# adaLN row sums by a reduction that turns 32 x 32 blocks on VectorE, and a group norm sum in single-pass products

## The chip, the cores and the metric

One core of one Trainium2 chip runs the whole program. The metric is device time in microseconds, lower is better. The kernel before took 1380.81 us, the median of 3 runs (1379.1 to 1381.97).

## What is computed

A trunk of two layers on x (512 tokens x 1024). Layer 0 mixes tokens with a gated short convolution, layer 1 with a Mamba-2 SSD mixer in 8 groups; a SwiGLU feed-forward layer (FFN) follows each. So there are four sub-layers, s = 0 to 3, and each is wrapped like this:

```
mod = (silu(c) @ ada_w + ada_b).reshape(bsz, DEPTH, 2, 3, D_MODEL)
shift, scale, gate = ...                            # of sub-layer s
h = rmsnorm(x, g_pre) * (1 + scale) + shift
x = x + gate * rmsnorm(mixer_or_ffn(h), g_post)
```

`ada_w` is 1024 x 12288 and c is one vector: a product of one row, whose 12288 results the kernel wants as columns (feature on partitions), 96 columns of 128 in `mods`. Inside the SSD mixer, y is normalised by groups of 256 features: `rms_normalize(y.reshape(bsz, s, g, 256))`. Everything is fp32.

## The kernel before

**Products.** All large products run as three single-pass products of 512 tokens each, on operands that are split in a high part (rounded to the reduced type fp32r) and the rest: lines 262, 263 and 264 of the input products, for example. ScalarE makes the high part of a weight and VectorE the rest (`split_w`, L202 and the line after it; L221 where the split is put later). A product of plain fp32 operands, as in the transposes of small things, the C-B products of the SSD and the sum of the group norm, is made of several passes by the compiler.

**Weights.** SP issues the loads of weights into a staging tile (`wst`, two buffers; L211 and L229), from which the two engines split them into `whl` (four buffers). At the end of each sub-layer, `load_lead` (L245) brings the first weights of the next one ("lead weights"), so that TensorE can start behind the boundary. The same SP queue issues the loads of `ada_w`.

**adaLN.** The first 16 columns of `mods` (shift and scale of sub-layer 0) come from products at the start (`ada_pe`, L184). The other 80 come from VectorE, in 20 sets of 512 columns of `ada_w` (`ada_set`). For a set, SP loads four tiles of 128 x 2 x 512 (`ada_st`, L134, three buffers); VectorE multiplies each 128 x 512 half by the value of silu(c) of its partition and adds it to an accumulator `ada_acc` (L124 the first, L126 the seven behind it; two buffers). What is left is a sum over the 128 partitions. `ada_finish` makes it: four transposes of 128 x 128 on TensorE (L119) put the accumulator into PSUM with features on partitions, and VectorE reduces over the free dimension (L120) and adds `ada_b`. `ada_fin` then makes the columns that are used: (1 + scale) times the pre-norm's weight (`acol`) and gate times the post-norm's (`gcol`). `ada_next(n)` finishes the set begun at the call before and begins n new ones. It is called with 2 in three of the four steps of the convolution layer, and 14 sets in all from nine steps of the first FFN; none is left behind that.

**Small vectors.** `other_vectors` loads four small vectors by rows with DMAs issued by ScalarE, and turns each into columns with a transpose (`ptr`, L91) and a copy. It is called in the third step of the convolution layer. `put_gates` (`ggp`) turns the gates of a sub-layer into rows; for sub-layers 1 to 3 that happens in the FFN's step f = 18.

**Group norm of the SSD.** For each of 8 groups, `step_c` makes two tiles `y0` of 128 features x 512 tokens. ScalarE squares each; VectorE adds the second square to the first (`accg`, L1133). `sums` lets TensorE sum `accg` over the partitions with a matrix of ones in plain fp32 (`ssg`, L1144), ScalarE takes the root (L1148), VectorE the reciprocal (L1152) and scales. `sums` stands about seven input products behind `step_c`.

**Order.** The instructions of each engine run in order. Mostly a scheduler places them, by the times at which it thinks buffers come free; so a buffer that is freed by another engine moves the loads behind it on SP, and the work on them.

**The boundary** at the end of a sub-layer: the last output products end, ScalarE squares (`xn<-y`, L411) the last rows, the norm follows, and TensorE turns the normalised rows (`xtr`, L478) into the next sub-layer's input. The lead weights' splits stand ahead of those squares on ScalarE.

Of the kernel before, what the change touches and what calls it, by code (L numbers as in the profile page):

```python
# [8 lines left out]
F32 = mybir.dt.float32  # L9
# [7 lines left out]
P = 128  # L17
T = 512
# [17 lines left out]
def trunk_kernel(  # L36
# [57 lines left out]
    def other_vectors(stage):  # L94
        d_rows = stage[:16, 3, :].rearrange("p (a b) -> p a b", b=HD)
        d16 = stage[:16, 4, 0:2]
        dma_s(stage[0:16, 0, :], m_norm_g.rearrange("i (r p) -> (i r) p", p=P))
        dma_s(stage[:32, 1, :], m_conv_b.rearrange("i (r p) -> (i r) p", p=P))
        dma_s(stage[:, 2, :], m_conv_w.rearrange("i k (r p) -> (i k r) p", p=P))
        dma_s(d16, m_d.rearrange("i (r p) -> (i r) p", p=2))  # L100
        turned(stage[:, 0, :], mng, 16)
# [3 lines left out]
        turned(d_rows.rearrange("p a b -> p (a b)"), dcol, 16)  # L105

    mods = consts.tile([P, 96], F32, name="mods")
    acol = consts.tile([P, 32], F32, name="acol")
# [2 lines left out]

    xt = [hp.tile([P, D], F32, name=f"x{t}", tag=f"x{t}") for t in range(4)]


    def ada_finish(acc, ncol, dst):
        n = ncol // P
        pt = aux_ps("ada_ps")
        for b in range(n):
            pe.transpose(pt[:, b * P:(b + 1) * P], acc[:, b * P:(b + 1) * P], ident)  # L119
        dve.tensor_reduce(dst, pt[:, :ncol].rearrange("p (a b) -> p a b", b=P), axis=AX.X, op=ADD)  # L120

    def ada_madd(acc, w, k):
        if k == 0:
# [12 lines left out]
                ada_madd(acc, st[:, k, :], kh * 2 + k)  # L136
        return acc

    def ada_fin(col0, acc):
# [4 lines left out]
        kind, j = divmod(r, 8)  # L144
        if kind == 1:
            dve.scalar_tensor_tensor(acol[:, s * 8 + j:s * 8 + j + 4], mods[:, q:q + 4], 1.0,
                                     ncol(s, 0, j, 4), ADD, MUL)
        elif kind == 2:
            dve.tensor_mul(gcol[:, s * 8 + j:s * 8 + j + 4], mods[:, q:q + 4], ncol(s, 1, j, 4))

    def ncol(s, post, j, n=1):
        i, sub = divmod(s, 2)
# [398 lines left out]
    ada_open = []  # L551
# [12 lines left out]
    with ExitStack() as ph:  # L564
        ada_p.append(ph.enter_context(tc.tile_pool(name="adap", bufs=3, reuse_waits="tile")))
        actp = ph.enter_context(tc.tile_pool(name="actp", bufs=22, reuse_waits="tile"))
        gx = ph.enter_context(tc.tile_pool(name="gx", bufs=1, reuse_waits="tile"))

        def act_tile(name):
            return actp.tile([P, 2, T], F32R, tag="a", name=name)  # L570
# [268 lines left out]
        def ffn(s, i, begun, act_tile, gg_tile, xn_tile, ada, gates, lead, after):  # L839
# [13 lines left out]
            for f in range(0, NF, 2):  # L853
# [9 lines left out]
                for b in range(2):  # L863
                    ff_act(pss[b], pss[2 + b], f + b)
                ada(f)
                if f == 18:
                    for q in gates:
                        put_gates(q)
                    gg = make_gg(s, gg_tile)
# [9 lines left out]
                    ssd_lead, lambda: load_w([(wm_in, P, P)]))  # L879
        h, lead_ps, rest, wz1 = begun  # L880

        assert not ada_sets and not ada_open


    with ExitStack() as ph:
# [99 lines left out]
        class Group:  # L985
# [120 lines left out]
            def step_c(self, q):  # L1106
# [23 lines left out]
                else:  # L1130
                    sqg = t2("sqg")
                    act.activation(sqg, y0, AF.Square)
                    dve.tensor_add(self.accg, self.accg, sqg)  # L1133
                ygs.append(y0)

            def step_d(self):
                self.sums()
                self.root()
                self.norm()

            def sums(self):

                self.ssg = aux_ps("ssg")
                pe.matmul(self.ssg, ones, self.accg, start=True, stop=True)  # L1144

            def root(self):
                self.rg = t2("rg")
# [34 lines left out]
        with tc.manual_schedule(engines={PE_ENGINE, mybir.EngineType.Activation, mybir.EngineType.DVE}):  # L1182
# [67 lines left out]
            next(conv2[3])  # L1250
            next(conv2[3])
            next(conv2[2])
            next(conv2[3])
            nn.split(1)
            nxt.project_z(0)
# [5 lines left out]
            for g in range(1, NG - 1):  # L1261
# [38 lines left out]
                if nn:  # L1300
                    nn.later[0][1]()
                    nn.split(1)
                next(conv2[3])
                nxt.project_z(0)
                if nn:
                    nn.weights(1)
# [81 lines left out]
```

## Time and profile before

| | |
|---|---|
| median of 3 runs | 1380.81 us |
| the profiled execution's own time | 1383.75 us |
| span of its profile | 1382.0 us |
| granted TensorE clock | 0.998 |
| opening, to the first product of the adaLN | 11.5 us |
| transposes of the first boundary (convolution layer to FFN) | from 206.3 us |
| first FFN | about 206 to 578 us |
| SSD layer's groups | 40.8 us from one group norm sum to the next |

The profile is of one execution, which had a time of its own; its span is what the trace covers, 1.75 us less. Times in the rows are in us from the span's start. PE is TensorE, PEld its weight loads, DVE VectorE, ACT ScalarE, POOL GpSimd, SP the engine that issues the loads. In a row of a group, `out<-in` names tiles (buffer numbers left out), `xN` is the number of instructions, and behind the bar stand busy time, mean ns of one, and the idle time ahead of them with what ended it. In a row of the timeline stand start, duration, engine, line, the operation and, in brackets, the idle time ahead of it and what ended it. Matmuls are pipelined, so their durations overlap; what one costs is read from the starts of its neighbours.

### The profile page before, as it was taken

To read this page: it belongs to the slowest core of one execution; us is meant where nothing else is said; L and a number is where in the kernel's file an instruction comes from. 1 tells how busy PE (TensorE), PEld (TensorE's weight loads), DVE (VectorE), ACT (ScalarE), POOL (GpSimd) and SP (SyncE) were. 2 spreads that over 40 slices of the span, in tenths; PEclk is the share of its full clock that TensorE was granted. 3 is DMA by queue.
4 is the path that set the end of the run, shared out by engine and by line. 5 is a ranking of instruction groups with operands and counts; after the bars stand their busy time and mean duration, and the time that the engine had idled before them with its cause. 6 is when DMAs were issued, how large, how long until landed. Compare 5 with 4: busy or idle time off the path is not lost.

```text
span 1382.0 us, 17400 instructions
## 1 busy us (share of the span) xinstructions
PE 1366.8 (99%) x7035; PEld 1147.2 (83%) x7035; DVE 841.6 (61%) x1331; ACT 535.4 (39%) x817; POOL 1.5 (0%) x11
## 2 busy tenths in 40 slices
PE   8999999999999999999999999999999999999998
PEld 7788879888888888898888888888888888888886
DVE  5887756487775222759988898897573333332224
ACT  5432256222222211745555445564472322222112
POOL 0000000000000000000000000000000000000000
PEclk9999999999999999999999999999999999999999
DMA  9966661368773223415343423313403223322221
GB/s 313 328 205 230 211 211 62 122 213 268 237 257 122 92 92 102 116 47 172 107 138 109 136 84 115 128 57 121 154 30 107 92 93 113 99 92 92 92 92 62
DMA packets 154181, 190.36 MB, mean 138 GB/s; under 512 B 5860, under 2 KB 111220, under 8 KB 153076
## 3 DMA queue, kind: packets, MB, share of 16 engines
q1 hardware_dynamic: 149952, 176.34, 39.8%
q10 hardware_dynamic: 4148, 12.90, 2.9%
q8 instruction: 55, 0.90, 0.3%
q14 instruction: 26, 0.21, 0.1%
HBM read 186.98 MB, written 2.24 MB: 137 GB/s over the span
## 4 chain that ended last, share of the span: by engine, by line
PE 65%; DMA 1%; DVE 1%; ACT 1%; issue 0%; DVEq 0%; ACTq 0%
PE ip L262 11%; PE ip L264 11%; PE ip L263 11%; PE y L362 7%; PE y L364 7%; PE y L363 7%; PE li L262 2%; PE li L264 2%; PE li L263 2%; PE yd L1118 1%; DMA wst<-in_f_w_in_dram 1%; PE yo L1112 1%; PE xtr L478 1%; PE cb L1057 1%; PE xtok L1040 1%; PE st L1073 0%
## 5 line engine op out<-in xcount | busy, mean ns | idle before, releaser
L262 PE MATMUL ip<-h,whl 128*128 128x512 f32 x1096 | 433.2, 395 | 0.0
L264 PE MATMUL ip<-h,whl 128*128 128x512 f32 x1096 | 427.2, 390 | 0.0
L263 PE MATMUL ip<-h,whl 128*128 128x512 f32 x1096 | 426.8, 389 | 0.0
L262 PEld LDWEIGHTS ip<-h,whl 128*128 128x128 f32 x1096 | 205.8, 188 | 44.1 <-issue 2.6
L263 PEld LDWEIGHTS ip<-h,whl 128*128 128x128 f32 x1096 | 205.9, 188 | 43.2 <-issue 1.4
L264 PEld LDWEIGHTS ip<-h,whl 128*128 128x128 f32 x1096 | 205.7, 188 | 43.3
L203 DVE TENSOR_TENSOR whl<-wst,whl 128x1024 fp32r<-128x1024 f32 (+1 forms) x127 | 133.5, 1070 | 105.9 <-ACT whl L202 105.7
L202 ACT CAST whl<-wst 128x1024 fp32r<-128x1024 f32 (+1 forms) x127 | 114.8, 926 | 202.6 <-PE ip L264 117.1
L203 DVE TENSOR_TENSOR whlo<-wsto,whlo 128x1024 fp32r<-128x1024 f32 x68 | 83.0, 1224 | 176.4 <-ACT whlo L202 176.2
L202 ACT CAST whlo<-wsto 128x1024 fp32r<-128x1024 f32 x68 | 71.2, 1051 | 197.5 <-PE y L364 158.8
L362 PE MATMUL y<-whlo,ff 128*128 128x512 f32 x352 | 137.0, 389 | 0.0
L364 PE MATMUL y<-whlo,ff 128*128 128x512 f32 x352 | 136.9, 389 | 0.0
L363 PE MATMUL y<-whlo,ff 128*128 128x512 f32 x352 | 136.9, 389 | 0.0
L126 DVE SCALAR_TENSOR_TENSOR ada_acc<-ada_st,csil,ada_acc 128x512 f32<-128x512 f32 x140 | 104.9, 749 | 20.0 <-DMA ada_st<-in_ada_w_dram 17.1
L262 PE MATMUL li<-h,whl 128*128 128x256 f32 x288 | 83.4, 290 | 0.0
L847 DVE TENSOR_TENSOR g<-ip,g 128x512 f32<-128x512 f32 x40 | 27.6, 690 | 90.2 <-PE ip L264 90.2
L264 PE MATMUL li<-h,whl 128*128 128x256 f32 x288 | 81.5, 283 | 0.0
L263 PE MATMUL li<-h,whl 128*128 128x256 f32 x288 | 81.5, 283 | 0.0
L846 ACT ACTIVATE g<-ip 128x512 f32<-128x512 f32 x36 | 21.5, 598 | 144.7 <-PE ip L264 144.7
L363 PEld LDWEIGHTS y<-whlo,ff 128*128 128x128 f32 x352 | 66.1, 188 | 13.8
L362 PEld LDWEIGHTS y<-whlo,ff 128*128 128x128 f32 x352 | 66.1, 188 | 13.7
L364 PEld LDWEIGHTS y<-whlo,ff 128*128 128x128 f32 x352 | 66.1, 188 | 13.6
(215 smaller groups left out, 1688.9 us busy)
## 6 DMA issues: line engine op xcount, KB each, us to landing
ada_st<-in_ada_w_dram SPq DMA_DIRECT2D x96, 512.0 KB, 5.7
wst<-in_f_w_in_dram SPq DMA_DIRECT2D x44, 1024.0 KB, 5.2
wsto<-in_f_w_out_dram SPq DMA_DIRECT2D x20, 1024.0 KB, 5.1
wst<-in_m_w_in_dram SPq DMA_DIRECT2D x14, 1024.0 KB, 5.3
wst<-in_m_w_in_dram SPq DMA_DIRECT2D x20, 512.0 KB, 4.2
wst<-in_a_w_in_dram SPq DMA_DIRECT2D x9, 1024.0 KB, 7.1
csb<-cs_d ACTq DMA_DIRECT2D x8, 1024.0 KB, 7.2
wsto<-in_m_w_out_dram SPq DMA_DIRECT2D x7, 1024.0 KB, 5.0
```

The costliest lines, as they stand in the source:

```text
L126: dve.scalar_tensor_tensor(acc, w, csil[:, k:k + 1], acc, MUL, ADD)
L202: act.copy(dst[:, 0, :nk, :], src)
L203: dve.tensor_tensor(dst[:, 1, :nk, :], src, dst[:, 0, :nk, :].bitcast(F32), SUB)
L262: pe.matmul(dst, w_at(w, 0, kk), a[:, 0, sl], start=start, stop=False)
L263: pe.matmul(dst, w_at(w, 0, kk), a[:, 1, sl], start=False, stop=False)
L264: pe.matmul(dst, w_at(w, 1, kk), a[:, 0, sl], start=False, stop=stop)
L362: pe.matmul(pst, a[:, 0, tk], wt[:, 0, kk, :], start=k == 0, stop=False)
L363: pe.matmul(pst, a[:, 0, tk], wt[:, 1, kk, :], start=False, stop=False)
L364: pe.matmul(pst, a[:, 1, tk], wt[:, 0, kk, :], start=False, stop=k == K - 1)
L478: pe.transpose(pt[:, j * 256 + t * P:j * 256 + (t + 1) * P], self.xn[2 * hi + t][p // 2][:, c:c + P], ident)
L846: act.activation(g, psg, AF.Silu)
L847: dve.tensor_mul(g, psu, g)
```

## The change

Three things are changed. Lines are those of the new kernel where the rows below are of it.

**adaLN.** `ada_finish` with its four transposes is gone. `ada_fold` reduces the accumulator on VectorE with `apply_transpose`: it views the 512 columns as 16 blocks of 32, turns each 32 x 32 block and sums it, so that row 32g + i, column b of the result holds the sum over the 32 partitions of quarter g, of accumulator column 32b + i. Two sets (1024 columns, one kind of one sub-layer) fill a tile `fold` of 128 x 32. What is left is the sum of four quarters: one plain fp32 product of `fold`, 32 columns, with `four`, a matrix that is 1 where row and column agree modulo 32 (four unit matrices added by GpSimd). Four additions of 32 partitions each put the result with `ada_b` into `mods`. `acol` and `gcol` are made for 8 columns at once instead of 4. `ada_next` finishes a pair of sets at the call behind the one that completed it.

**Small vectors.** `other_vectors` becomes a generator: its DMAs are issued in the convolution layer as before, its transposes stand in the first FFN at step f = 4. The gates of sub-layers 1 to 3 are put at f = 20 instead of 18.

**Group norm.** For groups 0 to 6 the second square is added by GpSimd instead of VectorE. `split_sq` splits `accg` as other operands are: ScalarE rounds it (`sqs`), VectorE takes the rest; and `sums` makes two single-pass products with `ones_r`, a rounded copy of the ones that ScalarE makes at the program's start. Group 7 stays as it was.

```diff
+    ones_r = consts.tile([P, P], F32R, name="ones_r")
+    act.copy(ones_r, ones)
...
-    def ada_finish(acc, ncol, dst):
-        n = ncol // P
-        pt = aux_ps("ada_ps")
-        for b in range(n):
-            pe.transpose(pt[:, b * P:(b + 1) * P], acc[:, b * P:(b + 1) * P], ident)
-        dve.tensor_reduce(dst, pt[:, :ncol].rearrange("p (a b) -> p a b", b=P), axis=AX.X, op=ADD)
...
+    def ada_fold(acc, dst):
+        dve.tensor_reduce(dst, acc.rearrange("p (b r) -> p b r", r=32), axis=AX.X, op=ADD, apply_transpose=True)
...
-        ada_finish(acc, 512, mods[:, q:q + 4])
-        dve.tensor_add(mods[:, q:q + 4], mods[:, q:q + 4], adab[:, q:q + 4])
+        pt = aux_ps("ada_ps")
+        pe.matmul(pt[:, :32], four, part, start=True, stop=True)
+        for b in range(4):
+            r = slice(b * 32, (b + 1) * 32)
+            dve.tensor_tensor(mods[r, q:q + KD], pt[r, :32].rearrange("p (q b) -> p q b", b=4)[:, :, b],
+                              adab[r, q:q + KD], ADD)
...
     def ada_next(n):
-        for _ in range(max(n, 1)):
-            if ada_open:
-                ada_fin(*ada_open.pop())
-            if ada_sets and n:
-                c0 = ada_sets.pop(0)
-                ada_open.append((c0, ada_set(c0)))
+        while ada_done:
+            ada_fin(*ada_done.pop())
+        for _ in range(n if ada_sets else 0):
+            c0 = ada_sets.pop(0)
+            if not ada_open:
+                ada_open.append((c0, small_p[0].tile([P, 32], F32, tag="fold", name="fold", bufs=2)))
+            i = (c0 - ada_open[0][0]) // 512
+            ada_fold(ada_set(c0), ada_open[0][1][:, i * 16:(i + 1) * 16])
+            if i:
+                ada_done.append(ada_open.pop())
...
-                other_vectors(actp.tile([P, 8, P], F32, tag="a", name="rows2"))
+                vectors = other_vectors(actp.tile([P, 8, P], F32, tag="a", name="rows2"))
+                next(vectors)
...
+                if f == 4 and s == 1:
+                    next(vectors)
-                if f == 18:
+                if f == 20:
...
-                    dve.tensor_add(self.accg, self.accg, sqg)
+                    if g < NG - 1:
+                        pool.tensor_tensor(self.accg, self.accg, sqg, ADD)
+                    else:
+                        dve.tensor_add(self.accg, self.accg, sqg)
...
+            def split_sq(self):
+                self.sqs = ysp.tile([P, 2, T], F32R, tag="ys", name="sqs")
+                hi, lo = self.sqs[:, 0, :], self.sqs[:, 1, :]
+                act.copy(hi, self.accg)
+                dve.tensor_tensor(lo, self.accg, hi.bitcast(F32), SUB)
...
-                pe.matmul(self.ssg, ones, self.accg, start=True, stop=True)
+                if self.g == NG - 1:
+                    pe.matmul(self.ssg, ones, self.accg, start=True, stop=True)
+                else:
+                    for i in range(2):
+                        pe.matmul(self.ssg, ones_r, self.sqs[:, i, :], start=i == 0, stop=i == 1)
```

**What moves.** First TensorE in the second step of the convolution layer, where the sets begun in the first one are finished (`h` is the layer's input, `ip` the product's PSUM tile). Before:

```order
L262 MATMUL ip<-h_299,whl 128x512
L263 MATMUL ip<-h_299,whl 128x512
L264 MATMUL ip<-h_299,whl 128x512
L119 MATMUL ada_ps<-ident,ada_acc 128x128 x8
L262 MATMUL ip<-h_112,whl 128x512
L263 MATMUL ip<-h_112,whl 128x512
```

The same place in the changed kernel:

```order
L269 MATMUL ip<-h_307,whl 128x512
L270 MATMUL ip<-h_307,whl 128x512
L271 MATMUL ip<-h_307,whl 128x512
L146 MATMUL ada_ps<-fold,four 128x32
L269 MATMUL ip<-h_120,whl 128x512
L270 MATMUL ip<-h_120,whl 128x512
```

Eight transposes, of two accumulators, have given way to one product on the fold tile of both; and the accumulators are no longer read by TensorE. Three such places stand ahead of the first boundary and seven in the first FFN.

Second SP, the queue of loads at the end of the convolution layer (`wsto` are the layer's output weights, L245 and L252 the three loads of the FFN's lead weights, L211 and L218 the FFN's other weights). Before:

```order
L134 DMA ada_st<-in_ada_w_dram 128x2x512 x4
L229 DMA wsto<-in_a_w_out_dram 128x4x512
L229 DMA wsto<-in_a_w_out_dram 128x2x512
L134 DMA ada_st<-in_ada_w_dram 128x2x512 x3
L229 DMA wsto<-in_a_w_out_dram 128x4x512
L134 DMA ada_st<-in_ada_w_dram 128x2x512
L245 DMA wst<-in_f_w_in_dram 128x8x256 x3
L211 DMA wst<-in_f_w_in_dram 128x8x256 x5
```

And in the changed kernel:

```order
L236 DMA wsto<-in_a_w_out_dram 128x2x512
L131 DMA ada_st<-in_ada_w_dram 128x2x512 x4
L236 DMA wsto<-in_a_w_out_dram 128x4x512
L131 DMA ada_st<-in_ada_w_dram 128x2x512 x2
L252 DMA wst<-in_f_w_in_dram 128x8x256
L131 DMA ada_st<-in_ada_w_dram 128x2x512 x3
L252 DMA wst<-in_f_w_in_dram 128x8x256 x2
L131 DMA ada_st<-in_ada_w_dram 128x2x512 x2
L218 DMA wst<-in_f_w_in_dram 128x8x256 x7
```

More loads of `ada_w` stand ahead of the last lead load: 49 instead of 35, counted from the program's start. They are loads that stood in the first FFN before.

Third VectorE in a group of the SSD layer, from the end of `step_c` to the next group's decay terms (`cu` is the convolution, `whl` a weight's split, `csb` the decay). Before:

```order
L1126 TENSOR_TENSOR yg_5772<-yg_5772,zs_5467 128x512
L1133 TENSOR_TENSOR accg<-accg,sqg 128x512
L977 SCALAR_TENSOR_TENSOR cu<-ip,cols_91,cu 128x511
L977 SCALAR_TENSOR_TENSOR cu<-ip,cols_91,cu 128x510
L977 SCALAR_TENSOR_TENSOR cu<-ip,cols_91,cu 128x509
L221 TENSOR_TENSOR whl<-wst,whl 128x1024 x3
L1089 TENSOR_SCALAR csb<-csb,cs_tok 128x128 x16
```

And in the changed kernel:

```order
L1147 TENSOR_TENSOR yg_5727<-yg_5727,zs_5421 128x512
L998 SCALAR_TENSOR_TENSOR cu<-ip,cols_93,cu 128x511
L998 SCALAR_TENSOR_TENSOR cu<-ip,cols_93,cu 128x510
L998 SCALAR_TENSOR_TENSOR cu<-ip,cols_93,cu 128x509
L228 TENSOR_TENSOR whl<-wst,whl 128x1024 x2
L1165 TENSOR_TENSOR sqs<-accg,sqs 128x512
L228 TENSOR_TENSOR whl<-wst,whl 128x1024
L1110 TENSOR_SCALAR csb<-csb,cs_tok 128x128 x16
```

The addition has left VectorE's row (it is GpSimd's now), and the subtraction that makes the rest of the squares stands three instructions later, between the splits of the weights.

More of the change, by code (lines that the diff above doesn't have):

```diff
@@ L137, in ada_set, with ada_fin @@
         return acc
[L139 removed]
+    def ada_fold(acc, dst):
+        dve.tensor_reduce(dst, acc.rearrange("p (b r) -> p b r", r=32), axis=AX.X, op=ADD, apply_transpose=True)
+    def ada_fin(col0, part):
         q = col0 // P
[L141 to L142 removed]
+        pt = aux_ps("ada_ps")
[4 more added lines that the diff above has]
+                              adab[r, q:q + KD], ADD)
         s, r = divmod(q, 24)
[L144 removed]
+        kind = r // 8
         if kind == 1:
[L146 to L147 removed]
+            dve.scalar_tensor_tensor(acol[:, s * 8:s * 8 + KD], mods[:, q:q + KD], 1.0, ncol(s, 0, 0, KD), ADD, MUL)
         elif kind == 2:
[L149 removed]
+            dve.tensor_mul(gcol[:, s * 8:s * 8 + KD], mods[:, q:q + KD], ncol(s, 1, 0, KD))
     def ncol(s, post, j, n=1):
@@ L567, in trunk_kernel @@
         gx = ph.enter_context(tc.tile_pool(name="gx", bufs=1, reuse_waits="tile"))
+        small_p.append(gx)
+        four = gx.tile([P, P], F32, tag="four", name="four", bufs=1)
+        pool.tensor_tensor(four[:, 0:64], ident[:, 0:64], ident[:, 64:128], ADD)
+        pool.tensor_tensor(four[:, 64:96], four[:, 0:32], four[:, 32:64], ADD)
+        pool.tensor_copy(four[:, 0:32], four[:, 64:96])
+        pool.tensor_copy(four[:, 32:64], four[:, 64:96])
+        pool.tensor_copy(four[:, 96:128], four[:, 64:96])
         def act_tile(name):
@@ L880, in trunk_kernel @@
         h, lead_ps, rest, wz1 = begun
-        assert not ada_sets and not ada_open
+        assert not ada_sets and not ada_open and not ada_done
     with ExitStack() as ph:
@@ L1252, in trunk_kernel @@
             next(conv2[2])
+            cur.split_sq()
             next(conv2[3])
```

9 lines of the change are left out of this document (4 added, 5 removed).

## The prediction

> **What bounds the kernel now.** I read the busy line of the page first, then the groups by line, then TensorE's waits. The groups' columns are busy time in us and mean ns of one, then the idle time ahead of them.
>
> ```profile
> PE 1366.8 (99%) x7035; PEld 1147.2 (83%) x7035; DVE 841.6 (61%) x1331; ACT 535.4 (39%) x817; POOL 1.5 (0%) x11
> ```
> ```profile
> L119 PE MATMUL ada_ps<-ident,ada_acc 128*128 128x128 f32 x80 | 10.8, 272 | 0.0
> L1144 PE MATMUL ssg<-accg,ones 128*128 128x512 f32 x16 | 8.2, 590 | 0.0
> ```
> ```profile
> PE xtr L478 <- ACT xn L469: 3.9, 4, 2.5
> ```
>
> TensorE is busy 99% of the span, and its largest wait is 3.9 us, at two of the boundaries between sub-layers. So work taken from TensorE's row shortens the program unless a new wait takes its place, and work on the other engines costs nothing until TensorE waits for it. The change touches both groups shown: 80 transposes of the adaLN sums, and 8 group-norm sums (16 records, since one fp32 product leaves two). Their busy figures overlap with neighbours, so I price them by starts in TensorE's timeline (start, duration, engine, line).
>
> ```profile
> 279.44 1.03 PE L119 MATMUL ada_ps<-ident,ada_acc 128*128 128x128 f32 x8
> 280.23 0.47 PE L262 MATMUL ip<-h,whl 128*128 128x512 f32 x1
> 280.54 0.39 PE L263 MATMUL ip<-h,whl 128*128 128x512 f32 x1
> ```
> ```profile
> 705.29 1.02 PE L1144 MATMUL ssg<-accg,ones 128*128 128x512 f32 x2
> 705.74 0.80 PE L262 MATMUL ip<-h,whl 128*128 128x512 f32 x1
> 706.38 0.40 PE L263 MATMUL ip<-h,whl 128*128 128x512 f32 x1
> ```
> ```profile
> 677.48 1.06 PE L1057 MATMUL cb<-ct,bt 128*128 128x128 f32 x8
> 678.29 0.48 PE L262 MATMUL ip<-h,whl 128*128 128x512 f32 x1
> 678.60 0.39 PE L263 MATMUL ip<-h,whl 128*128 128x512 f32 x1
> ```
> ```profile
> 131.41 0.39 PE L262 MATMUL ip<-h,whl 128*128 128x512 f32 x1
> 131.73 0.23 PE L91 MATMUL ptr<-ident,rows 16*128 16x16 f32 x1
> 131.89 0.50 PE L263 MATMUL ip<-h,whl 128*128 128x512 f32 x1
> 132.23 0.39 PE L264 MATMUL ip<-h,whl 128*128 128x512 f32 x1
> ...
> 133.06 0.39 PE L263 MATMUL ip<-h,whl 128*128 128x512 f32 x1
> 133.29 0.27 PE L91 MATMUL ptr<-ident,rows 128*128 128x128 f32 x1
> 133.31 0.48 PE L264 MATMUL ip<-h,whl 128*128 128x512 f32 x1
> 133.63 0.39 PE L262 MATMUL ip<-h,whl 128*128 128x512 f32 x1
> 133.86 0.40 PE L263 MATMUL ip<-h,whl 128*128 128x512 f32 x1
> ```
>
> A single-pass product of 512 columns takes 0.23 us (133.63 to 133.86). Eight transposes with the product behind them take 280.54 - 279.44 = 1.10 us, so the eight cost 0.87, or 0.109 each. A group-norm sum takes 706.38 - 705.29 = 1.09 less 0.23 = 0.86. Four fp32 products of 128 columns cost 1.12 - 0.23 = 0.89, or 0.22 each. A turn of a small vector costs 132.23 - 131.41 less two products = 0.36, the 128-row one 133.63 - 133.06 less two = 0.11.
>
> **The change, part by part, on TensorE.** *adaLN:* 80 transposes go, 80 x 0.109 = 8.7 us: 24 of them (2.6) ahead of the first boundary at 206 us, 56 (6.1) in the first FFN. Ten fp32 products with 32 columns come, 3 and 7. No row shows that shape; it lies between one transpose, 0.11, and the 128-column product, 0.22. I take 0.2, since it also loads 128 x 128 weights twice: +0.6 and +1.4. *Small vectors:* 3 x 0.36 + 0.11 = 1.2 us are moved from ahead of the boundary to behind it. *Group norm:* seven of the eight sums become two single-pass products, 7 x (0.86 - 2 x 0.23) = 2.8 us less, behind the boundary.
>
> *Opening:* ScalarE gets a table load and a small copy (ones_r) ahead of two DMA issues and of its own chain.
>
> ```profile
> 2.65 1.28 ACT L679 ACT_TABLE_LOAD   x1 [2.65 <-issue]
> ```
> ```profile
> 5.90 0.29 ACT L633 ACTIVATE ss<-ss,eps 128x1 f32<-128x1 f32 x1 [0.24 <-DVE xn L622]
> ```
> ```profile
> 11.53 0.64 PE L184 MATMUL ada_pe<-ada_st,rows 128*32 128x128 f32 x16 [1.11 <-DMA ada_st<-in_ada_w_dram]
> ```
>
> With the copy priced as that square root, it comes 1.28 + 0.29 less its 0.24 of idle time, some 1.3 us, later. What hides it is TensorE's wait for the first weights at 11.53, 1.11 us long. I take +0.2, between 0 and 1.3.
>
> So ahead of the boundary TensorE has 2.6 - 0.6 + 1.2 - 0.2 = 3.0 us less, behind it 6.1 - 1.4 - 1.2 + 2.8 = 6.3 us less.
>
> **What the boundary does with the 3.0.** The boundary at the end of the convolution layer waits for ScalarE.
>
> ```profile
> 195.64 2.18 ACT L202 CAST whl<-wst 128x512 fp32r<-128x512 f32 x4 [1.48 <-DMA wst<-in_f_w_in_dram]
> 197.72 0.59 ACT L411 ACTIVATE xn<-y 128x512 f32<-128x512 f32 x1
> ```
> ```profile
> 205.07 0.39 PE L364 MATMUL y<-whlo,bu 128*128 128x512 f32 x1
> 206.29 0.33 PE L478 MATMUL xtr<-ident,xn 128*128 128x128 f32 x1 [0.84 <-ACT xn L469]
> ```
>
> ScalarE starts the boundary's squares at 197.72, the moment its splits of the last lead weights end, and these waited for their DMA until 195.64. TensorE's transposes at 206.29 hang on that chain. A TensorE that comes 3 us sooner only waits 3 us longer, unless this load comes sooner as well. Does it? The accumulator is now freed by VectorE's own reduction instead of by TensorE's transposes, and the order on SP and VectorE moves with it: ahead of the last lead load stand 49 loads of ada_w instead of 35, and ahead of the boundary on VectorE 96 multiply-adds instead of 64. The rows for that stretch, and for one in the first FFN (length, then PE, PEld, DVE, ACT and POOL busy, clock, DMA share, GB/s):
>
> ```profile
> 57.00:198.00 141.00, 141.00 (x634) 116.06 (x633) 105.72 (x156) 44.72 (x60) 0.00 (x0) 1.00 0.68 225
> ```
> ```profile
> 302.10:324.80 22.70, 22.70 (x106) 18.88 (x105) 19.50 (x29) 6.32 (x8) 0.00 (x0) 1.00 0.85 286
> ```
> ```profile
> L126 DVE SCALAR_TENSOR_TENSOR ada_acc<-ada_st,csil,ada_acc 128x512 f32<-128x512 f32 x52 | 38.9, 748 | 6.7 <-DMA ada_st<-in_ada_w_dram 5.7
> ...
> L120 DVE TENSOR_REDUCE mods<-ada_ps 128x4 f32<-128x512 f32 x6 | 3.9, 680 | 0.0
> L124 DVE TENSOR_SCALAR ada_acc<-ada_st,csil 128x512 f32<-128x512 f32 x7 | 3.4, 479 | 0.0
> ```
>
> Four more sets are 4 x (0.48 + 7 x 0.75) = 22.9 us of VectorE. Ten reductions, for now priced as the old ones, stand where six stood, +2.7, and the small additions and the vectors' copies about cancel: 105.7 becomes 131 of 141 us, or of 138 if TensorE is to come 3 us sooner. Waits for ada_w, 5.7 us for 59 instructions, grow to about 9 for 91 (96 less the five ahead of 57 us). That is 140 of 138: VectorE is full, and it makes the splits that free the buffer of the last lead load. The transfers fit: 14 loads of 128 x 2 x 512 fp32, 0.52 MB, in 141 us raise 225 to 277 GB/s, and at 286 GB/s TensorE was busy 22.70 of 22.70. So I let the load land when it did, and count the 3.0 as lost. The bounds of this term are 3.0 (and up to 0.8 more, the wait itself) gained, and 8 lost, which is what VectorE falls behind if its waits double.
>
> In the first FFN fewer sets are left, 8 instead of 12, and the densest steps had two sets each, as now. VectorE's 40 additions of 32 x 8 and the reductions lie beside TensorE there, as 19.5 busy of 22.7 us did.
>
> **What hides the group norm's new steps.** The sum of squares moves to GpSimd, then ScalarE rounds it and VectorE subtracts; TensorE waits for that.
>
> ```profile
> 697.05 0.63 ACT L1132 ACTIVATE sqg<-yg 128x512 f32<-128x512 f32 x1 [1.75 <-DVE yg L1126]
> ...
> 700.72 0.63 ACT L979 ACTIVATE ct<-cu 128x512 f32<-128x512 f32 x1 [2.10 <-DVE cu L977]
> ```
> ```profile
> 697.71 0.69 DVE L1133 TENSOR_TENSOR accg<-accg,sqg 128x512 f32<-128x512 f32 x1 [0.70 <-ACT sqg L1132]
> ...
> 709.28 3.35 DVE L1152 RECIPROCAL rg<-rg 128x512 f32<-128x512 f32 x1 [2.10 <-ACT rg L1148]
> ```
> ```profile
> 1.77 0.29 POOL masks.py:66 TENSOR_SCALAR_AFFINE_SELECT mask<-mask 128x128 f32<-128x128 f32 x1
> ```
>
> GpSimd's addition of 512 columns is shown nowhere. The nearest rows are VectorE's, 0.69, and GpSimd's own select of 128 columns, 4 x 0.29 = 1.2, which I take as an estimate. It runs from 697.7 to 698.9. ScalarE's copy stands behind ct, which comes 1.4 us sooner since VectorE no longer waits and adds (700.72 to 699.3), so it ends near 700.5; VectorE subtracts behind two splits, by 702.2, and TensorE asks at 705.29. Three us are left, so the price is nothing. The queue behind the wait is the next z gate's silu on ScalarE and a split on VectorE, and VectorE has 2.10 us idle ahead of 709.28. The cover is gone if the addition takes about 5 us, and then each us beyond it costs seven.
>
> [...]
>
> **Sum.** -6.3 behind the boundary and 0 ahead of it: 1383.75 - 6.3 = 1377.4 for the profiled execution (span 1382.0 and 1.75 around it). That execution lies 2.9 us above the median of 1380.81, so against the median it is 1374.5.
>
> **The rivals.** *All of it comes through:* VectorE and the loads follow TensorE, and the boundary starts 3.0 us sooner or loses its wait: 1370.7 to 1371.5. Against it stands the full VectorE.
>
> *VectorE or the loads fall further behind* in the convolution layer, through longer waits for ada_w, and the boundary starts 3 to 8 us late: 1377.5 to 1382.5.
>
> *Slower: the reduction that turns 32 x 32 blocks costs more than a plain one.* Its price is in no row; 0.68 is that of a reduction that turns nothing. Ten stand ahead of the boundary on a VectorE without room, so each us more than 0.68 puts the boundary 10 us later. It decides at 0.68 + 6.3/10 = 1.3 us: there the gain is gone. At four times the plain price, 2.7 us, the boundary is 20 us late and the time 1395. [...]
>
> *The sum waits in the SSD layer:* an addition of 7 us on GpSimd gives 7 x 1 to 7 x 3 us of wait, 1381 to 1395.
>
> **How the numbers follow.** The forecast, the boundary within 2 us of where it was, has 0.5 (1372.5 to 1376.5). All comes through 0.17, falling further behind 0.2, the dear reduction 0.1, the waiting sum 0.03. A measurement of this kernel tells 0.2%, 2.8 us, from no change. Faster than 1378.0 are the first two and a little of the third: 0.70. Most of the third is within 0.2%: 0.17. Slower: 0.13. The range from 1369.5 to 1382 takes in the bounds of the products, of the opening and most of the third case, and leaves out the last two.
>
> **What would show it.** In the groups, 20 records of the new product instead of 80 transposes, at about 0.2 us a product by starts; a sum's place of 0.45 instead of 0.86, so that seven periods of the SSD layer are 0.4 us shorter each; TensorE's wait at the first boundary grown from 0.84 to near 4 us, with ScalarE's lead splits still ending near 197.7; the turned reduction near 0.7 us. The forecast is wrong if TensorE waits for splits ahead of 190 us, if the first boundary's transposes start outside 204 to 208.5 us, or if the reduction or GpSimd's addition is several times its price.

## The result, and the profile after

The changed kernel took 1380.45 us, the median of 12 runs (1378.07 to 1383.53), the kernel before 1380.66 us (12 runs); the ratio is 0.9994 with a 95% interval of 0.9985 to 1.0004. The forecast was 1374.5 us. Nothing that can be measured came of it, though everything that was to be taken from TensorE's row was taken. Against the first trace of before, TensorE's busy time fell by 10.1 us, but its idle time grew from 15.2 to 22.5 us; the 2.8 us between the two spans is no gain, since that first execution lay 3.1 us above its median. First the page's busy line of the changed kernel, then its groups (busy, mean ns | idle ahead):

```profile
PE 1356.7 (98%) x6975; PEld 1141.1 (83%) x6975; DVE 842.9 (61%) x1344; ACT 540.9 (39%) x826; POOL 11.6 (1%) x23
```
```profile
L139 DVE TRANSPOSE_TENSOR_REDUCE fold<-ada_acc 128x16 f32<-128x512 f32 x20 | 13.5, 694 | 0.0
L1155 POOL TENSOR_TENSOR accg<-accg,sqg 128x512 f32<-128x512 f32 x7 | 9.1, 1299 | 893.2 <-ACT sqg L1153 893.2
L149 DVE TENSOR_TENSOR mods<-ada_ps,cols 32x8 f32<-32x8 f32 x40 | 6.4, 160 | 0.4
```

The prices that no row of before had are shown here: the turned reduction takes 0.69 us, GpSimd's addition 1.30 us. TensorE's waits in the changed kernel (total, times, longest):

```profile
PE y L369 <- DVE mods L149: 8.3, 1, 8.3
PE ada_pe L191 <- DMA ada_st<-in_ada_w_dram: 3.0, 3, 1.5
PE xtr L485 <- ACT xn L476: 1.6, 2, 1.3
```

The first is new. It stands at the start of the convolution layer's output products, and what follows is as telling as the wait. TensorE's timeline there:

```profile
161.20 0.30 PE L146 MATMUL ada_ps<-fold,four 128*128 128x32 f32 x2
...
163.04 0.39 PE L370 MATMUL y<-whlo,bu 128*128 128x512 f32 x1
163.27 0.40 PE L371 MATMUL y<-whlo,bu 128*128 128x512 f32 x1
171.98 0.77 PE L369 MATMUL y<-whlo,bu 128*128 128x512 f32 x1 [8.31 <-DVE mods L149]
172.54 0.63 PE L370 MATMUL y<-whlo,bu 128*128 128x512 f32 x1
172.97 0.63 PE L371 MATMUL y<-whlo,bu 128*128 128x512 f32 x1
```

The output products want a PSUM tile that last held the third fold's product. It is free when VectorE's four additions (`mods`, L149) have read it. That product (L146) ran at 161.20 us; VectorE's row shows why the additions came ten us later:

```profile
162.68 0.75 DVE L123 SCALAR_TENSOR_TENSOR ada_acc<-ada_st,csil,ada_acc 128x512 f32<-128x512 f32 x1
163.35 0.68 DVE L823 TENSOR_TENSOR u_cv<-ip,u_cv 128x512 f32<-128x512 f32 x1
163.95 0.74 DVE L123 SCALAR_TENSOR_TENSOR ada_acc<-ada_st,csil,ada_acc 128x512 f32<-128x512 f32 x1
164.61 1.22 DVE L210 TENSOR_TENSOR whlo<-wsto,whlo 128x1024 fp32r<-128x1024 f32 x1
165.74 0.68 DVE L825 TENSOR_TENSOR bu<-u_cv,bu 128x512 fp32r<-128x512 f32 x1
166.34 0.74 DVE L123 SCALAR_TENSOR_TENSOR ada_acc<-ada_st,csil,ada_acc 128x512 f32<-128x512 f32 x1
169.10 1.54 DVE L123 SCALAR_TENSOR_TENSOR ada_acc<-ada_st,csil,ada_acc 128x512 f32<-128x512 f32 x2 [2.01 <-DMA ada_st<-in_ada_w_dram]
170.55 0.68 DVE L823 TENSOR_TENSOR u_cv<-ip,u_cv 128x512 f32<-128x512 f32 x1
171.15 0.68 DVE L149 TENSOR_TENSOR mods<-ada_ps,cols 32x8 f32<-32x8 f32 x4
```

VectorE runs its row in order, without a gap but the one of 2.01 us for a load of ada_w, and is behind. The multiply-adds in it are of sets that the kernel before made behind the boundary. The stretches (length, then PE, PEld, DVE, ACT and POOL busy, clock, DMA share, GB/s), and VectorE's multiply-adds from 57 to 198 us:

```profile
57.00:198.00 141.00, 132.69 (x581) 109.38 (x580) 122.63 (x184) 41.32 (x52) 0.00 (x0) 0.98 0.82 263
...
172.00:175.50 3.50, 3.50 (x8) 2.76 (x9) 3.50 (x7) 0.00 (x0) 0.00 (x0) 0.50 0.41 142
...
180.00:216.00 36.00, 34.42 (x153) 28.05 (x151) 28.05 (x49) 17.52 (x40) 0.00 (x0) 1.00 0.85 283
```
```profile
L123 DVE SCALAR_TENSOR_TENSOR ada_acc<-ada_st,csil,ada_acc 128x512 f32<-128x512 f32 x78 | 57.7, 745 | 12.5 <-DMA ada_st<-in_ada_w_dram 11.5
...
L121 DVE TENSOR_SCALAR ada_acc<-ada_st,csil 128x512 f32<-128x512 f32 x11 | 5.2, 473 | 3.3 <-DMA ada_st<-in_ada_w_dram 3.3
```

89 multiply-adds instead of 59, and 14.8 us of waiting for ada_w instead of 5.7. Behind the wait the granted clock is 0.50 for 3.5 us, and the products there stand 0.43 us apart instead of 0.23 (172.54 to 172.97). At the boundary the lead weights come late as well (ScalarE's row):

```profile
204.60 2.18 ACT L209 CAST whl<-wst 128x512 fp32r<-128x512 f32 x4 [1.31 <-DMA wst<-in_f_w_in_dram]
206.69 0.59 ACT L418 ACTIVATE xn<-y 128x512 f32<-128x512 f32 x1
```

The squares that started at 197.72 now start at 206.69, again the moment the splits end, and TensorE's transposes come at 215.38 instead of 206.29:

```profile
215.38 0.33 PE L485 MATMUL xtr<-ident,xn 128*128 128x128 f32 x1 [1.29 <-ACT xn L476]
```

The wait there is 1.29 us, where before it was 0.84: nearly all of the delay was there already, from the wait at 163 us. Behind the boundary the gain runs about as forecast. One group norm sum of the changed kernel:

```profile
709.62 0.39 PE L271 MATMUL ip<-h,whl 128*128 128x512 f32 x1
709.85 0.61 PE L1174 MATMUL ssg<-sqs,ones_r 128*128 128x512 f32 x2
710.30 0.39 PE L269 MATMUL ip<-h,whl 128*128 128x512 f32 x1
```

The two products take 0.45 us (709.85 to 710.30). So the question was what makes the convolution layer lose the 9 us: the PSUM tile, VectorE's work, the loads, or all the order brought forward.

### The profile page after: what moved, and what is told of

Its sections match the earlier page's. It is cut to its first block, busy times and chain, and to the rows that moved or that the text cites. A ratio compares the mean times of both kernels' runs of the same rounds, so it can differ in the third digit from the quotient of the medians.

```text
span 1379.2 us, 17320 instructions
## 1 busy us (share of the span) xinstructions
PE 1356.7 (98%) x6975; PEld 1141.1 (83%) x6975; DVE 842.9 (61%) x1344; ACT 540.9 (39%) x826; POOL 11.6 (1%) x23
## 4 chain that ended last, share of the span: by engine, by line
PE 84%; DVE 6%; DMA 6%; SPq 1%; issue 1%; ACT 1%; DVEq 0%; ACTq 0%
PE ip L269 16%; PE ip L271 16%; PE ip L270 16%; PE y L369 8%; PE y L371 8%; PE y L370 8%; DMA ada_st<-in_ada_w_dram 4%; PE li L269 3%; PE li L271 3%; PE li L270 3%; DVE ada_acc L123 2%; PE yd L1139 1%; DMA wst<-in_f_w_in_dram 1%; DVE whl L210 1%; PE yo L1133 1%
```

## The experiments

**Theory:** the accumulators are freed by VectorE itself, so the order brings later sets ahead of the boundary; VectorE and the loads fall behind, and whatever TensorE wants of VectorE there comes late. **Rivals:** only the PSUM tile is badly placed; or only the loads count; or the gain behind the boundary isn't real. All kernels in one table: multiply-adds on VectorE ahead of the third fold's additions and ahead of the boundary, and loads of the sets on SP ahead of the last lead load (counted in the order of the instructions; where expectations speak of 51 or 65 loads, the opening's 16 are in it); from the trace, TensorE's longest wait between 150 us and the boundary's end, and the start of the boundary's transposes; then the median and the ratio to before with its interval. The ratio is to the kernel before in the same session, where its median was 1380.66 us for the changed kernel, 1380.52 for E1 to E4, 1380.16 for E5 to E7 and 1379.49 for E9 to E12; medians of different sessions are compared only roughly.

| | adds ahead | loads | wait | transposes | median | ratio |
|---|---|---|---|---|---|---|
| before (second trace, E8) | -, 64 | 35 | 0.7 | 206.02 | | |
| changed | 78, 96 | 49 | 8.3 | 215.38 | 1380.45 | 0.9994 (0.9985 to 1.0004) |
| E1 norm only | -, 64 | 35 | 1.3 | 207.07 | 1376.45 | 0.9971 (0.9962 to 0.998) |
| E2 ScalarE frees | 80, 96 | 49 | 7.6 | 218.69 | 1377.87 | 0.9984 (0.9969 to 0.9999) |
| E3 held from 9 | 64, 64 | 35 | under 0.3 | 203.76 | 1367.76 | 0.991 (0.9896 to 0.9923) |
| E4 ones late | 78, 96 | 49 | 8.5 | 213.29 | 1380.93 | 0.9998 (0.999 to 1.0007) |
| E5 tile not used | none there, 96 | 49 | 3.2 | 212.43 | 1379.41 | 0.999 (0.9979 to 1.0001) |
| E6 no loads | 80, 96 | 32 | 4.6 | 209.86 | 1374.66 | 0.9956 (0.9939 to 0.9972) |
| E7 short adds | 80, 96 | 50 | 3.9 | 208.69 | 1376.42 | 0.9964 (0.9952 to 0.9977) |
| E9 one fold tile | 64, 80 | 42 | 2.7 | 205.44 | 1372.7 | 0.9945 (0.993 to 0.996) |
| E10 held from 11 | 78, 80 | 43 | 10.4 | 215.92 | 1379.11 | 0.9995 (0.9986 to 1.0004) |
| E11 held from 7 | 48, 48 | 27 | under 0.3 | 201.96 | 1367.02 | 0.991 (0.9894 to 0.9927) |
| E12 held, old norm | 64, 64 | 35 | under 0.3 | 202.48 | 1370.19 | 0.993 (0.9916 to 0.9945) |

**E1, the group norm alone.** The kernel before with these lines of the change: `ones_r`, GpSimd's addition, `split_sq` and the two products.

```diff
+                    if g < NG - 1:
+                        pool.tensor_tensor(self.accg, self.accg, sqg, ADD)
...
+            cur.split_sq()
```

> Kernel before plus the group norm's part of the change alone. Both theories have the seven sums at 0.45 us each by starts instead of 0.86 and GpSimd's addition at 1.3 us; the SSD groups then lie 40.35 us apart instead of 40.81. Theory A (the group norm's gain reaches the end): 2.8 to 3.2 us faster than before, about 1377.5. Theory B (the boundary behind the SSD layer waits for its own loads and takes the gain back): TensorE waits some 3 us longer at that boundary and the time is within 1 us of before, about 1380.5. In both the first boundary's transposes stay at 206 us, since the convolution layer is the old one.

4.1 us faster: theory A, and somewhat more than it gave; its trace has a TensorE wait of 1.3 us at most at any boundary, where the first trace of before has 2.5. The sums of E1:

```profile
L1155 PE MATMUL ssg<-sqs,ones_r 128*128 128x512 f32 x14 | 4.3, 389 | 0.0
L1152 PE MATMUL ssg<-accg,ones 128*128 128x512 f32 x2 | 1.0, 590 | 0.0
```

So the loss is not in this part.

**E2, ScalarE frees the PSUM tile.**

```diff
+        sb = small_p[0].tile([P, 32], F32, tag="fsum", name="fsum", bufs=2)
+        act.copy(sb, pt[:, :32])
...
-            dve.tensor_tensor(mods[r, q:q + KD], pt[r, :32]...
+            dve.tensor_tensor(mods[r, q:q + KD], sb[r, :32]...
```

> Changed kernel, but ScalarE copies the fold product out of PSUM and VectorE adds from the copy, so the PSUM tile that the output products want is no longer freed by VectorE. Theory A (that wait, 8.3 us at 163 us, and the slow products behind it are what the convolution layer loses): the wait is gone, no products at 0.43 us, the first boundary's transposes at 204 to 208 us instead of 215, time 1371 to 1374. Theory B (VectorE and the loads of ada_w that stand ahead of the lead weights set the boundary by themselves): the wait is gone as well, but TensorE waits elsewhere, the transposes stay at 213 to 216 us and the time at 1379 to 1381.

Neither came true: the wait stayed and only changed its owner.

```profile
PE y L371 <- ACT fsum L148: 7.6, 1, 7.6
PE xtr L487 <- ACT xn L478: 3.7, 2, 3.5
```

ScalarE's copy stands in its row behind steps that wait for VectorE (`bu` waited 3.38 us for it) and behind a split that waited 3.47 us for its load. It didn't tell the theories apart; E5 was made for that. (Its trace is of an execution of 1385.09 us, the longest of its runs.)

**E3, the later sets held behind the boundary.** Sets from the ninth on use a copy of silu(c) that depends on the new x:

```diff
+    cs_now = [csil]
...
-            dve.scalar_tensor_tensor(acc, w, csil[:, k:k + 1], acc, MUL, ADD)
+            dve.scalar_tensor_tensor(acc, w, cs_now[0][:, k:k + 1], acc, MUL, ADD)
...
+                if f == 4 and s == 1:
+                    cs2 = consts.tile([P, KD], F32, name="csil2")
+                    dve.scalar_tensor_tensor(cs2, xt[0][:, 0:KD], 0.0, csil, MUL, ADD)
+                    cs_now[0] = cs2
```

> Changed kernel, but the sets from the ninth on take silu(c) from a copy that is made only behind the first boundary, so that 64 multiply-adds stand ahead of that boundary on VectorE as before, not 96, and 64 not 78 ahead of the third fold's additions. Theory A (VectorE is behind because the order brings later sets forward): the wait at 163 us falls under 1 us, the first boundary's transposes come at 203 to 207 us, time 1370 to 1373. Theory B (the four small additions that read PSUM are badly placed whatever stands ahead): the wait stays at 6 us or more, time 1378 to 1381. Theory C (the boundary is gained, but the held sets crowd the first FFN): transposes at 203 to 207 us, but the FFN no longer 4 us shorter, time 1374 to 1378.

Theory A, and beyond its range: 1367.76 us. In the held kernel VectorE reads the PSUM tile at once, and is busy 4.5 of 11 us where the changed kernel had 8.9 and still was late:

```profile
161.52 0.69 DVE L825 TENSOR_TENSOR u_cv<-ip,u_cv 128x512 f32<-128x512 f32 x1 [0.38 <-PE ip L273]
162.13 0.68 DVE L151 TENSOR_TENSOR mods<-ada_ps,cols 32x8 f32<-32x8 f32 x4
```
```profile
161.00:172.00 11.00, 11.00 (x51) 9.11 (x50) 4.52 (x10) 2.62 (x3) 0.00 (x0) 1.00 0.33 101
```

VectorE waits more for ada_w than in the kernel before, 10.1 us between 57 and 198 us instead of 5.7 (7.2 in the second trace, E8), and TensorE loses 0.3 us at most by it (busy 140.67 of 141.00 us there): with as few multiply-adds as before VectorE has the room.

```profile
L125 DVE SCALAR_TENSOR_TENSOR ada_acc<-ada_st,csil,ada_acc 128x512 f32<-128x512 f32 x52 | 38.5, 745 | 10.8 <-DMA ada_st<-in_ada_w_dram 10.1
```

From the boundary's last transpose to the FFN's output products TensorE gained 4.2 us in both the changed and the held kernel, so the held sets don't crowd the FFN.

**E4, the copy of the ones later.**

```diff
-    act.copy(ones_r, ones)
...
         cs_d = dram.tile([NH, T], F32, name="cs_d")
+        act.copy(ones_r, ones)
```

> Changed kernel, but the rounded copy of the ones is made at the start of the SSD layer, so that ScalarE has no table load and copy among its first DMA issues. The trace of the changed kernel has TensorE's products 1.2 to 1.7 us later than before at 50 to 60 us. Theory A (that is the price of the copy at the start): the products at 50 us come as early as before, 0 to 0.4 us later; the time is at most 1.7 us below the changed kernel, and about the same if the wait at 163 us takes it up. Theory B (the loads at the start differ from run to run): the products at 50 us lie anywhere from 0 to 1.7 us late, and the time is that of the changed kernel, 1380.5.

The time is that of the changed kernel. At 54 us TensorE is 0.05 us behind the first trace of before, but with the copy it was 0.3 behind in E1, 1.7 in the changed kernel, 1.2 in E3 and nothing in E11: theory B, the copy has no price that can be seen. These differences at the opening are part of each trace's time at the boundary.

**E5, the PSUM tile isn't used there.** The third pair is finished in the FFN, and three fold tiles keep the order at 96 multiply-adds and 49 loads. The scale column that this pair would have given is set to 1 instead, so the results are not the reference's.

```diff
+    pool.memset(acol[:, 8:16], 1.0)
...
-            ada_next(2 if jp < 6 else 0)
+            if jp < 6:
+                ada_next(2)
```

> Changed kernel, but the third pair of sets is finished in the first FFN, so the PSUM tile that the output products want at 163 us is not used at all there; the first FFN then reads a scale column of 1 instead of the computed one. VectorE has 96 multiply-adds and SP 65 loads of ada_w ahead as in the changed kernel. Theory A (the PSUM tile held behind VectorE's backlog is what the convolution layer loses): no wait at 163 us, first boundary's transposes at 203 to 208 us, time 1368 to 1373. Theory B (the backlog and the loads set the boundary by themselves, the PSUM wait only shows it first): the wait at 163 us is gone, but TensorE waits later in the output products or at the boundary, transposes at 211 to 216 us, time 1376 to 1381.

Theory B. The wait at 163 us is gone and comes back in pieces, for splits of weights and at the boundary:

```profile
PE xtr L486 <- ACT xn L477: 3.4, 2, 3.2
...
PE y L371 <- DVE whlo L211: 2.3, 2, 1.3
PE y L370 <- ACT whlo L210: 1.9, 1, 1.9
```

The PSUM tile was only where TensorE met VectorE's lag first. The transposes come 3.0 us sooner than in the changed kernel, but 1.5 of that was there at 60 us already, and at the FFN's end the two traces differ by that 1.5 alone (582.1 and 583.6 us). The medians, 1379.41 and 1380.45, are not told apart.

**E6 and E7, the work without the loads, and the loads without the work.** E6 multiplies the unit matrix in the later sets; E7 cuts all their multiply-adds but the first to 64 columns. Neither computes the reference's modulation.

```diff
+        if nset[0] > 8:
+            src = ident.unsqueeze(1).to_broadcast([P, 4, P])
...
+                n = 64 if nset[0] > 8 and kh * 2 + k else 512
+                ada_madd(acc[:, :n], st[:, k, :n], kh * 2 + k)
```

> Changed kernel, but the sets from the ninth on multiply the unit matrix instead of loaded tiles, so their loads are left out and the modulation of the later sub-layers is not the reference's. VectorE still has 96 multiply-adds ahead of the first boundary, 80 ahead of the third fold's additions; SP has 48 loads of ada_w ahead of the last lead load instead of 65. Theory A (VectorE's own work ahead of the additions makes the wait): it stays at 5 us or more, time 1376 to 1381. Theory B (the loads that those multiply-adds wait for make it): the wait falls under 2 us, transposes at 203 to 207 us, time 1366 to 1372.

> Changed kernel, but in the sets from the ninth on all multiply-adds but the first cover 64 columns instead of 512, so the modulation of the later sub-layers is not the reference's. All loads are as in the changed kernel, and the order has 80 multiply-adds ahead of the third fold's additions, of which those of the later sets are short, about 0.2 us instead of 0.75. Theory A (VectorE's own work): the wait at 163 us falls under 2 us and the time to 1366 to 1373. Theory B (the loads that stand ahead and are waited for): the wait stays at 5 us or more, time 1376 to 1381.

Neither theory's wait in either: each half alone leaves about half of it. First E6, then E7:

```profile
PE y L377 <- DVE mods L157: 4.6, 1, 4.6
```
```profile
PE y L372 <- DVE mods L152: 3.9, 1, 3.9
```

E6's VectorE is busy 10.9 of the 11 us from 161 to 172 with little to wait for; in E7 it waits 13.1 us for ada_w between 57 and 198 us with 52 us of multiply-adds instead of 63 (the short ones took some 0.28 us each: 46.4 us for 80, less 38.5 for 52 full ones as E6 has them). VectorE's work and the loads it waits for both count.

**E8, the kernel before once more** (no edit).

> The kernel before once more, for a second trace of it. Its first profiled execution took 1383.75 us, some 3 us over the median, with TensorE waiting 2.5 us at the boundary behind the SSD layer. Theory A (that wait is of this one execution): the second one has less than 1 us there and takes about 1381. Theory B (the kernel before always waits there): 2 us or more again, and a part of what the group norm's change gains is this wait.

Theory A, though faster than it gave: a trace of an execution of 1378.77 us, in which TensorE's products differ from the first by under 0.8 us up to the boundary behind the SSD layer, and the first trace loses 4.6 us there. That boundary in the first trace, and in the second (ScalarE's row):

```profile
997.22 2.19 ACT L202 CAST whl<-wst 128x512 fp32r<-128x512 f32 x4 [1.66 <-DMA wst<-in_f_w_in_dram]
```
```profile
993.79 2.19 ACT L202 CAST whl<-wst 128x512 fp32r<-128x512 f32 x4 [0.79 <-DMA wst<-in_f_w_in_dram]
```

In the first the last lead load landed 3.4 us later, TensorE waited 2.5 us, and some products behind ran at half rate (0.43 us apart, 1008.51 to 1008.94). Only one of the two executions shows it; so the second trace is the better measure of where time went. Its first transposes:

```profile
206.02 0.33 PE L478 MATMUL xtr<-ident,xn 128*128 128x128 f32 x1 [0.69 <-ACT xn L469]
```

Why that load landed late in the first execution stays open.

**E9, one fold tile instead of two.**

```diff
-                ada_open.append((c0, small_p[0].tile([P, 32], F32, tag="fold", name="fold", bufs=2)))
+                ada_open.append((c0, small_p[0].tile([P, 32], F32, tag="fold", name="fold", bufs=1)))
```

> Changed kernel, but with one fold tile instead of two. The order then has 64 multiply-adds ahead of the third fold's additions (78 in the changed kernel) and 80 ahead of the first boundary (96), 58 loads of ada_w ahead of the last lead load (65). Theory A (the boundary follows all that is brought ahead of it): no wait at 163 us, but the boundary's transposes at 206 to 211 us, half way between the changed kernel and the held one, time 1370 to 1376. Theory B (only what stands ahead of the additions counts): transposes at 203 to 205 us, time 1366 to 1369. Theory C (the backlog builds up before that and stays): wait of 4 us or more, time 1377 to 1381.

Theory A's time, 1372.7, though the transposes start at 205.44: with 64 multiply-adds ahead of the additions there is no wait at 163 us, but the 80 ahead of the boundary are paid there, in a wait of 2.7 us:

```profile
PE xtr L485 <- ACT xn L476: 2.7, 1, 2.7
```

**E10, held from the eleventh set on** (`f == 6` instead of `f == 4` in E3's edit).

> Held kernel, but only from the eleventh set on: 78 multiply-adds ahead of the third fold's additions as in the changed kernel, 80 ahead of the boundary, 59 loads of ada_w ahead of the last lead load. Theory A (the backlog ahead of the additions makes the wait, and VectorE has no room behind it to win it back): the wait at 163 us stays at 6 to 9 us, the boundary's transposes at 210 to 215 us, time 1376 to 1381. Theory B (the work and loads between 163 us and the boundary make the delay): transposes at 206 to 209 us, time 1370 to 1374.

Theory A, a little beyond its bounds. As many multiply-adds ahead of the boundary as in E9, but 78 instead of 64 of them ahead of the additions, and the wait is back:

```profile
PE y L371 <- DVE mods L151: 10.4, 1, 10.4
```

**E11, held from the seventh set on** (`f == 0` in E3's edit).

> Held kernel, but from the seventh set on: 48 multiply-adds ahead of the boundary and 43 loads of ada_w ahead of the last lead load, fewer than the kernel before had (64 and 51). Theory A (TensorE bounds the held kernel already): the time is that of the held kernel, 1367 to 1369. Theory B (the first FFN has 14 sets to make and VectorE or the loads fall behind there): 1370 to 1378, with waits of TensorE between 206 and 460 us.

Theory A: 1367.02 us, and no crowding with all 14 sets in the FFN. The boundary comes 1.8 us sooner than in E3, but 1.3 of that was there at 60 us, ahead of the held sets, and the medians differ by 0.7 us, which these runs don't tell apart.

**E12, held with the old group norm** (E3's edit without the group norm's lines).

> Held kernel with the group norm of the kernel before: the adaLN's part and the moved small vectors alone. By the traces TensorE has some 3 us less ahead of the first boundary and 4 us less in the first FFN. Theory A (both parts add): 7 to 9 us faster than before, 1371.5 to 1373.5. Theory B (the boundary behind the SSD layer, where executions of the kernel before wait from 0 to 2.5 us, eats part of it): 3 to 6 us faster, 1374.5 to 1377.5.

1370.19 us, 9.3 us faster than before: more than either theory. With the 4.1 us of E1 the two parts make 13.4, E3 has 12.8 with both: within the spread of the runs they add.

## Why the prediction was wrong, step by step

**TensorE's row: right.** A fold's product cost 0.24 us with what it adds to its neighbours (0.2 forecast), the sums 0.45 instead of 0.86. The folds' plain fp32 products left two records each (20 for ten), as the old sums did (16 for eight), but the transposes only one (80 for 80, at 0.109 us against 0.22 for such a product of as many columns): the records show several passes for the products, not for the transposes. From the second trace of before to that of the changed kernel, TensorE is 9.4 us late at the boundary, 5.4 at the FFN's end and 2.2 at the last group's sum: 4.0 and 3.2 us gained, 7.2 behind the boundary where I forecast 6.3. The excess is in the small vectors, where three turns in a row cost 0.40 us together, and in the sums (3.2 for 2.8).

**The new prices: right.** The turned reduction is 0.694 us, against 0.680 for the plain reduction of as many columns, so the rival of a dear reduction falls. GpSimd's addition took 1.30 us for the 1.2 taken, and no sum waited. All seven additions lay beside `cu` instructions and none beside a split (the second from 702.39 to 703.68 us, with `cu` from 701.49 and the next split at 703.72), so what an addition and a split cost side by side was not shown.

**The step that failed** is the one at the boundary: "So I let the load land when it did, and count the 3.0 as lost." I had VectorE full (140 of 138 us), and that was so: 122.6 us busy and 14.8 us of waits for ada_w, with work left over. But a full engine in front of an end isn't neutral. I took the old landing, a row of a VectorE with room, as the nearest one, and put the loss, 8 us, only at the edge of the range.

What the runs showed in its place is a delay of 9.4 us at the boundary. In the trace of the changed kernel, 1.8 us of it, against the second trace of before, were there at 60 us (E4). TensorE made them good and came to the output products 1.5 us sooner than before; the wait at 163 us and the slow products behind it took 10.3 us, and the boundary's own wait grew by 0.6 only. So the load of the last lead weights, on which I put the whole question, was not where this trace lost its time; in E5, without the wait at 163 us, the boundary's own comes to 3.2 us. Four things went into the delay:

- VectorE's work and the loads it waits for, 32 multiply-adds and 14 loads more than before. E3, which holds them back, has no wait; E6 and E7, with one half of it each, have 4.6 and 3.9 us. "The transfers fit", read from TensorE's row, did not hold for VectorE: with the loads and short multiply-adds the 3.9 stay.
- The waits for ada_w, which I let grow by 3.3 us. They grew by 9.1, or by 7.6 from the second trace of before; on a VectorE with room (E3) waits of 10.1 us cost TensorE 0.3 us at most.
- I looked at VectorE's splits alone and not at what else it frees, the PSUM tile, where TensorE first met the lag. I counted the small additions as VectorE's time only. E5 shows that the tile decides where the loss is seen and little of how much it is.
- A wait that long (8.3 us) cost some 1.8 us more here, since the products behind it ran at half clock (0.50 for 3.5 us).

That the scheduler brings the sets forward because the accumulators come free sooner was my argument and is not shown; the order shows only that it did, and E9, where one fold tile fewer leaves 80 instead of 96, is in line with it.

**The rivals.** "VectorE or the loads fall further behind", which I gave 0.2, is what happened: 9.4 us, or 7.6 without what was there at 60 us, at the upper end of my 3 to 8, and a time within its 1377.5 to 1382.5. "All of it comes through" is E3 and E11: as soon as the order holds the later sets back, the boundary comes 2.3 to 4.1 us sooner than in the second trace of before, where I had 3.0 and up to 0.8. **The opening** cost nothing that can be told from the spread of the loads there. **The median** of before lies 1.9 us above the second trace's own time, likely since some executions of before wait at the SSD layer's boundary; part of the 12.8 us that E3 gains is likely that wait (the two spans differ by 10.1), but this was not tried by itself. And the 3.9 us that I called TensorE's largest wait was the sum of four; the longest, 2.5, was this one.

So the sum of -0.2 us is: some 9 us late at the boundary, most of it by an order that nobody wrote, against 7 us gained behind it and some 2 us between the medians and these two traces, likely the wait that some executions of before have at the SSD layer's boundary.

## What to carry to other kernels

When a change frees a buffer sooner, ask what a scheduler will put into the room, and on which engine's row: here 32 multiply-adds and 14 loads moved ahead of a boundary and ate a gain of 10 us, and one false dependency that held them back (E3) gave 1367.8 us, a ratio of 0.991 (0.9896 to 0.9923). An engine that comes out full in the sum of a stage is a forecast of delay, not of no change; look at everything that it frees for the bound engine, small things too. And read a wait as where the lag shows: taking that wait away (E5) gained nothing that these runs tell from the changed kernel, while taking away what stood ahead of it (E3) gained 12.7 us.

## What the runs showed of the hardware

Behind 60 us the traces have ten gaps of 2.86 us or more between two starts on TensorE, and behind each of them 3 to 12 products ran at half rate (0.427 us apart instead of 0.227); after gaps of 1.0 to 1.8 us that stood alone none did. In E5 three gaps followed each other within 7 us, of 1.3, 2.3 and 1.8 us, and seven products behind them ran at half rate. The first trace of before shows it from 1004 us on, where an idle time of 2.5 us cost some 1.6 us more behind it. Behind the 8.3 us wait of the changed kernel the granted clock was 0.50 for 3.5 us (172.0 to 175.5); in other runs the slow stretch lasted from some 2.9 us (E10) to 5.7 (E6), by the products' starts. The shortest gaps with products at half rate behind them were 2.86 us (before, first trace) and 3.05 us (E9).
